# A decoder step on one core: two plain feed-forward tiles instead of three, right factors made in order of use, a norm's end counted in products, and one POOL product pinned in place

## The chip, the cores and the metric

The kernel runs on one core of a Trainium2 chip. The metric is the device time of one execution in microseconds (us). Five engines work side by side, each through its own list of instructions in a fixed order: TensorE (PE, with its weight loads shown as PEld), VectorE (DVE), ScalarE (ACT), GpSimd (POOL) and SyncE (SP), which starts the transfers.

## The reference, cut to what matters

One step of a two-layer decoder over 1024 prompt tokens and 8 decode rows (1032 columns), width 1024, everything in float32:

```python
for l in range(2):
    xn = modulate(h, norm_w[l, 0], sh1, sc1)         # rms_norm(h) * (1 + scale) + shift
    if l == 0:
        mix, s_new = hgrn2_mixer(xn, ...)            # gated linear recurrence, 8 heads
    else:
        mix = sliding-window attention over the shared K/V
    h = h + g1 * mix
    xn = modulate(h, norm_w[l, 1], sh2, sc2)
    h = h + g2 * swiglu(xn, w_ffn_in[l], w_ffn_out[l])   # d_ff = 2816
    if l == 0:
        k_sh, v_sh = modulate(h, kv_norm_w, ...) @ w_kv  # shared by layer 1
y = rms_norm(h, final_norm_w)
```

For a decode row, a head of the recurrence does `s_new = f * s + k v^T` on its 128 x 128 state, and its output is the query times that state.

## The kernel before, in words

**Products.** A float32 matrix product is made of three matmuls (`mm3`, L283 to L285) of operands split in a rounded high part and a low rest. A weight comes by a transfer to a `raw` buffer; ACT casts it (L182, the high part) and POOL subtracts (L185, the rest). The pairs stand in a ring of `RING = 8` units of 512 columns; most tiles are two units, and `ws.next()` writes the conversion of up to three tiles ahead of the one in use. The activations are split in the same way.

**Columns.** A layer's columns are worked through in chunks: four of 258 (`G4`) for the feed-forward's input side and the output projection, three of 344 (`G3`) for the rest.

**Feed-forward (`ffn`).** There are 22 tiles of 128 hidden channels, each with a gate and an up part. The first `PLAIN` tiles are plain products: two tiles together, chunk by chunk as each chunk of the normalised input becomes ready (`need`), and any further plain tile after them. The remaining tiles use seven products of half-size blocks in place of eight (`seven_products`, in the order 1, 2, 6, 7, 5, 3, 4). Their right factors (`xs7`) are blocks of the input (1, 2, 3) or sums of such blocks (4 to 7), which `factors` makes: `diff` subtracts two blocks on DVE (L1393), `part` splits the result (ACT cast L1388, DVE subtraction L1389). They overwrite the residual's stack `f`.

**A norm's end.** While the last products of a sub-layer run, each chunk's squares are summed (`square`: L783, L786, and L788 on DVE or POOL). `finish(c, before, after)` merges them on DVE (L801), lets `before` steps go by, sums over the partitions on PE (L714), takes the inverse root on DVE and makes a diagonal (L720), lets `after` steps go by and spreads it over the partitions on PE (L729). `apply_steps` then scales rows (L809), adds scale and shift on ACT, and splits (ACT, DVE L837). These pieces stand as generators in the list `later`; after each product the code calls `step()`, which takes the next piece of the first generator in the list that has real work, and also one of every generator that only counts (`LAG`). `flush` empties the list.

**Heads.** `run` interleaves generators by weights: while head h+1's projections (`hgrn_proj`) run, the core of head h (`hgrn_core`) runs beside them. A core goes through levels M = 1, 2, ... 64: PE (L1043, L1089, L1110), then DVE on queries and keys (L1064, L1065). `vb` is the decode rows' v, spread over the partitions by a round trip through DRAM (`vsc`), and POOL multiplies it with k (L1125). Later the decode states are updated (L1146), the outputs normalised (L1198), gated and sent to `osc` (L1214). The last head's core runs beside `wo_first`, the half of the output projection that needs heads 0 to 3; `conditioning` (L473) runs there too. `wo_first` takes four weight tiles at once, eight units. `wo_second` follows; it needs heads 4 to 7, loaded and split by `mixed` (L1301, L1302, L1304).

**Order.** The Python code gives a program order. A planner orders each engine's list ahead of the run from that order and from when it reckons operands to be ready, so a piece that is ready early can stand earlier than it was written. `tc.keep_in_program_order(i)` pins an instruction behind the last one that was written before it for its engine.

The K/V norm (`ToKV`) ends in the same way during the feed-forward's output products; `nkv.apply_steps` runs a second time to make the queries' input during the K/V products.

Of the kernel before, what the change touches and what calls it, by code (L numbers as in the profile page):

```python
# [12 lines left out]
ALU = mybir.AluOpType  # L13
# [4 lines left out]
P = 128  # L18
D = 1024
KT = 8  # L20
T = 1024
NB = 8
Q = 86
TOK = T + NB
# [6 lines left out]
RING = 8  # L31
RAW = 3
NSLOT = 34
PLAIN = 3
MAGIC = 0x5F3759DF


# [16 lines left out]
G3, G4 = Grid(344), Grid(258)  # L54
# [3 lines left out]
def bc(ap, axis, n):  # L58
    u = ap.unsqueeze(axis)
    shape = list(u.shape)  # L60
    shape[axis] = n
    return u.to_broadcast(shape)
# [3 lines left out]
def trunk_kernel(  # L66
# [40 lines left out]
    pe, act, dve, pool, sp = nc.tensor, nc.scalar, nc.vector, nc.gpsimd, nc.sync  # L107
# [14 lines left out]
    def big(dt=F32, cols=TOK, parts=P):  # L122
        return p4.tile([parts, cols], dt, tag="c4", name=nm("c4"))
# [14 lines left out]
    def small(shape, tag, bufs=2, dt=F32):  # L138
        return sm.tile(shape, dt, tag=tag, name=nm(tag), bufs=bufs)
# [74 lines left out]
    def ntile(w, n0):  # L214
        ws.add(
            split_unit(
                [
                    (
                        lambda r: r.rearrange("p (k n) -> p k n", k=KT),
                        w[:, n0 : n0 + P].rearrange("(k p) n -> p k n", p=P),  # L220
                    )
                ]
            ),
            2,
        )
# [6 lines left out]
    def seven(w, j):  # L232
        box = {}

        def load():
            for i in range(2):
                raw = wraw()
                v = raw.rearrange("p (g k n) -> p g k n", g=2, k=4)
                for g in range(2):
                    src = w[i * 512 : (i + 1) * 512, g * DFF + j * P : g * DFF + (j + 1) * P]  # L240
                    sp.dma_start(v[:, g], src.rearrange("(k p) n -> p k n", p=P))
                box[0, i] = raw[:, 0:512]
                box[1, i] = raw[:, 512:1024]

        def first():
            load()
            a11, a12, a21, a22 = box[0, 0], box[0, 1], box[1, 0], box[1, 1]
            u = weight(a11)
            s3 = wp.tile([P, 512], F32, tag="s3", name=nm("s3"), bufs=1)
            box["s3"] = s3  # L250
            dve.tensor_tensor(s3, a11, a21, op=ALU.subtract)
            dve.tensor_tensor(a21, a21, a22, op=ALU.add)
            dve.tensor_tensor(a11, a21, a11, op=ALU.subtract)
            return u

        def last_sum():
            s = box[0, 0]
            dve.tensor_tensor(s, box[0, 1], s, op=ALU.subtract)
            return weight(s)

        ws.add(first)
        ws.add(lambda: weight(box[0, 1]))
        ws.add(lambda: weight(box[0, 0]))
        ws.add(lambda: weight(box["s3"]))
        ws.add(lambda: weight(box[1, 0]))
        ws.add(last_sum)
        ws.add(lambda: weight(box[1, 1]))
# [71 lines left out]
    def ffn_units(l):  # L339
        for j in range(PLAIN):  # L340
            ntile(w_ffn_in[l], j * P)
            ntile(w_ffn_in[l], DFF + j * P)
        for j in range(PLAIN, NF):
            seven(w_ffn_in[l], j)
        for j in range(2):
            ktile(w_ffn_out[l], j)
        for j in range(2, NF, 4):
            for np_ in range(4):
                wo_pair(w_ffn_out[l], j, np_)
# [56 lines left out]
    for kk in range(4):  # L406
        t = big(cols=1024)
        wa[0].append(first_half(2 * kk, 0, t))
        t = big(cols=1024)
        wa[0].append(first_half(2 * kk + 1, 0, t))  # L410
    ws.ahead(3)
    for k in range(4):
        t = big(cols=1024)
# [141 lines left out]
    LAG = "lag"  # L555
# [4 lines left out]
        later.append([g, next(g) == LAG])  # L560

    def step(n=1):
        for _ in range(n):
            worked = False
            for e in list(later):
                if worked and not e[1]:
                    break
                r = next(e[0], None)
                if r is None:
                    later.remove(e)  # L570
                    continue
                e[1] = r == LAG
                worked = worked or not e[1]
# [56 lines left out]
    class Stack:  # L630
# [12 lines left out]
        def part(self, c, i, n):  # L643
            r = self.rows(i)
            return self.t[c][i][:, : r.stop - r.start, :n]
# [204 lines left out]
    def residual_dec(tdec):  # L850
        dve.tensor_tensor(hd, hd, tdec, op=ALU.add)


    N = Norm()
# [34 lines left out]
    for half in range(2):  # L889
# [5 lines left out]
            op=ALU.mult,  # L895
# [115 lines left out]
    def hgrn_core(hh):  # L1011
        f, kk, v, q, g = data.pop(hh)
# [5 lines left out]
        for half in range(2):  # L1018
            ps = axp()
            for j in range(4):  # L1020
                c = 4 * half + j
# [8 lines left out]
        vb = big(cols=T).rearrange("p (b v) -> p b v", b=NB)  # L1030
# [87 lines left out]
        for half in range(2):  # L1118
            ps = axp()
            for j in range(4):  # L1120
                c = 4 * half + j
                pe.transpose(ps[:, j * P : (j + 1) * P], KS[:, c * P : (c + 1) * P], ident)
            act.copy(kt[:, half * 512 : (half + 1) * 512], ps)

        pool.tensor_tensor(vb, vb, bc(kk[:, T:TOK], 2, P), op=ALU.mult)  # L1125
        yield
        S = big(cols=T)
        for half in range(2):
# [4 lines left out]
            for j in range(4):  # L1133
                c = 4 * half + j
# [25 lines left out]
        for half in range(2):  # L1160
            ps = axp()
            po.append(ps)
            for j in range(4):
                c = 4 * half + j
# [5 lines left out]
            for j in range(4):  # L1170
                c = 4 * half + j
# [25 lines left out]
        for half in range(2):  # L1197
# [4 lines left out]
                op=ALU.mult,  # L1202
# [4 lines left out]
        for half in range(2):  # L1207
            ps = axp()
            for j in range(4):
                c = 4 * half + j  # L1210
# [119 lines left out]
    def wo_second(o, gate, m, back, beside=iter(())):  # L1330
        tdec = small([P, KT, NB], "tdec", 2)
        us = [ws.next() for _ in range(4)]
        st = res[-1]
        N = StackNorm(st)
        x = Quads()

        def then(c):
            st.move(back, [c], False)
            yield from N.finish(c, *((3, 8) if c < G4.last else (2, 4)))
            yield LAG  # L1340
            yield from N.apply_steps(c, m, x)

        for c in range(G4.n):
            for n in range(KT):
                wo_product(us[n // 2], o, c, n, gate, tdec, G4, anyp)
                N.square(c, n)
                step()
                if c and ((c - 1) * KT + n) % 2 == 0:
                    next(beside, None)
            if c == G4.last:  # L1350
                residual_dec(tdec)
                N.square_dec()
            queue(then(c))
        for _ in beside:
            pass
        return x, st
# [18 lines left out]
    def factors(x, st):  # L1375

        x = x.q
        f = st.t  # L1380
        xs7 = [{1: x[2 * i][0], 2: x[2 * i][1], 3: x[2 * i + 1][1]} for i in range(2)]

        def flat(t):
            return t.rearrange("p k n -> p (k n)")

        def part(raw):
            xh, xl = quad()
            act.copy(xh, raw)  # L1388
            dve.tensor_tensor(xl, raw, xh, op=ALU.subtract)  # L1389
            return xh, xl  # L1390

        def diff(p, q, dst):
            dve.tensor_tensor(flat(dst), flat(p), flat(q), op=ALU.subtract)  # L1393
            return dst

        def steps():
            t2 = []
            for i in range(2):
                b11, b12, b22 = f[2 * i][0], f[2 * i + 1][0], f[2 * i + 1][1]
                t1 = diff(b12, b11, b11)  # L1400
                yield
                xs7[i][5] = part(t1)
                yield
                t2.append(diff(b22, t1, t1))
                yield
                xs7[i][6] = part(t2[i])
                yield
            for i in range(2):
                t3 = diff(f[2 * i + 1][1], f[2 * i + 1][0], f[2 * i + 1][0])
                yield  # L1410
                xs7[i][7] = part(t3)
                yield
            for i in range(2):
                t4 = diff(f[2 * i][1], t2[i], t2[i])
                yield
                xs7[i][4] = part(t4)
                yield

        return xs7, steps()

    def ffn(l, x, st, hs, norm, aside=None):
# [3 lines left out]
        xs7, prepare = factors(x, st)  # L1425

        def prepare_all():
            for _ in prepare:
                yield 1

        later.append([prepare_all(), False])

# [14 lines left out]
        for c in range(G4.n):  # L1447
            need(x, c)
            for i in range(2):
                gate(ui[2 * i], c, sg[i])  # L1450
                step()
                up(ui[2 * i + 1], c, sg[i])
                step()
        for i in range(2):
            sp.dma_start(act_out[i], sg[i])
        for j in range(2, PLAIN):
            sg = big()
# [71 lines left out]
        ready = []  # L1529
# [8 lines left out]

        for j in range(PLAIN, NF):
            if j == NF // 2 and aside:  # L1540
# [57 lines left out]
    class ToKV(StackNorm):  # L1598
# [12 lines left out]

        def then(self, c):
            self.st.move(hsc, [c], False)
            yield from self.finish(c, 3, 5)
            yield LAG
            yield from self.apply_steps(c, 2, self.x, keep=True)

# [9 lines left out]
    for c in range(NCH):  # L1627
        need(nkv.x, c)
        for n in range(4):
            ps = mmp()  # L1630
            proj(ps[:, :W], us[n], nkv.x, c)
            act.copy(kvT[n][:, G3.cs[c] : G3.cs[c] + W], ps[:, :W])
            step(2)
        later.append([nkv.apply_steps(c, 3, X, first=False), False])
    kT, vT = kvT[:2], kvT[2:]

# [2 lines left out]
    for a in range(2):  # L1639
        t = big(cols=T)  # L1640
# [411 lines left out]
```

## Time and profile before

| what | value |
|---|---|
| median of 3 runs | 2527.67 us (2525.5 to 2528.7) |
| profiled execution | 2529.57 us, span 2527.8 us |
| mean granted clock of TensorE | 0.992 |
| PE busy | 2469.5 us, 98% |
| DVE, ACT, POOL busy | 1366.9, 878.7, 797.3 us |

The span is the time between the first and the last instruction in the trace of the profiled execution; that execution's own time is the figure beside it. An engine's row gives the sum of its busy time. In timelines a row is: start, duration, engine, line, operation, output <- inputs, shape, and in brackets how long the engine stood idle just before and who ended that.

### The profile page before, as it was taken

What the parts mean: (1) busy time and instruction counts of PE and PEld (TensorE: products, weight loads), DVE (VectorE), ACT (ScalarE), POOL (GpSimd) and SP (SyncE); (2) the same over time, 40 slices, a digit from 0 to 9 for tenths busy, and PEclk for the clock granted to TensorE, in tenths of its full rate; (3) what the DMA queues carried; (4) which work ended last, traced back from release to release, by engine and by line L of the source; (5) the groups of instructions that cost most, each with busy time, mean ns of one, the idle gap of its engine ahead of it and who ended that gap; (6) DMA issues with size and microseconds to landing.
All of it is one profiled execution on the core that took longest, in us unless ns stands there. A gap on an engine that the chain in (4) does not pass through costs nothing.

```text
span 2527.8 us, 52251 instructions
## 1 busy us (share of the span) xinstructions
PE 2469.5 (98%) x21579; PEld 2346.0 (93%) x21579; DVE 1366.9 (54%) x3117; ACT 878.7 (35%) x1929; POOL 797.3 (32%) x577
## 2 busy tenths in 40 slices
PE   7999999999999999999999999999899999999998
PEld 4989999987889999999999997878899999999998
DVE  5444555564574555656433725566845555555436
ACT  4323333331363332333211655454633333333112
POOL 2211222220334444444432231102334444445321
PEclk9999999999999999999999999999999999999999
DMA  8564222248942223226321322523222222264201
GB/s 317 188 213 138 72 78 69 69 149 286 284 126 78 81 85 116 89 89 229 123 76 54 89 55 59 155 88 109 76 70 82 84 76 76 76 230 145 69 26 68
DMA packets 314495, 293.41 MB, mean 116 GB/s; under 512 B 28617, under 2 KB 291674, under 8 KB 314226
## 3 DMA queue, kind: packets, MB, share of 16 engines
q1 hardware_dynamic: 313856, 289.86, 35.5%
q8 instruction: 170, 2.79, 0.4%
q14 instruction: 67, 0.55, 0.1%
q10 hardware_dynamic: 402, 0.22, 0.0%
HBM read 231.27 MB, written 63.99 MB: 117 GB/s over the span
## 4 chain that ended last, share of the span: by engine, by line
PE 89%; DVE 5%; DMA 2%; issue 2%; SPq 1%; ACT 0%; POOL 0%; DVEq 0%; POOLq 0%; ACTq 0%
PE mm L283 20%; PE mm L285 20%; PE mm L284 20%; PE ax L283 6%; PE ax L284 6%; PE ax L285 6%; PE ax L473 2%; PE ax L1798 1%; PE ax L1869 1%; PE ax L1043 1%; PE ax L1855 1%; DVE c L1064 1%; PE ax L1132 1%; PE ax L1169 1%; DVE hs L809 1%
## 5 line engine op out<-in xcount | busy, mean ns | idle before, releaser
L185 POOL TENSOR_TENSOR wu<-raw,wu 128x512 fp32r<-128x512 f32 x460 | 626.2, 1368 | 1354.8 <-ACT wu L182 1118.7
L283 PE MATMUL mm<-c,wu 128*128 128x344 f32 (+1 forms) x2096 | 669.9, 320 | 6.0 <-ACT c L742 4.1
L285 PE MATMUL mm<-c,wu 128*128 128x344 f32 (+1 forms) x2096 | 658.7, 314 | 1.7 <-POOL wu L185 1.7
L284 PE MATMUL mm<-c,wu 128*128 128x344 f32 (+1 forms) x2096 | 658.7, 314 | 0.1
L182 ACT CAST wu<-raw 128x512 fp32r<-128x512 f32 x460 | 283.3, 620 | 705.9 <-PE mm L285 377.0
L283 PEld LDWEIGHTS mm<-c,wu 128*128 128x128 f32 x2096 | 395.6, 189 | 20.0 <-issue 10.3
L283 PE MATMUL mm<-xq,wu 128*128 128x258 f32 x1448 | 412.2, 285 | 1.0 <-ACT wu L182 1.0
L285 PE MATMUL mm<-xq,wu 128*128 128x258 f32 x1448 | 409.9, 283 | 0.8 <-POOL wu L185 0.8
L284 PE MATMUL mm<-xq,wu 128*128 128x258 f32 x1448 | 410.3, 283 | 0.0
L285 PEld LDWEIGHTS mm<-c,wu 128*128 128x128 f32 x2096 | 395.6, 189 | 6.2 <-issue 4.1
L284 PEld LDWEIGHTS mm<-c,wu 128*128 128x128 f32 x2096 | 396.2, 189 | 4.3 <-issue 3.4
L283 PE MATMUL ax<-xq,wu 128*128 128x258 f32 x1064 | 301.4, 283 | 0.0
L284 PE MATMUL ax<-xq,wu 128*128 128x258 f32 x1064 | 300.9, 283 | 0.0
L285 PE MATMUL ax<-xq,wu 128*128 128x258 f32 x1064 | 300.6, 283 | 0.0
L285 PEld LDWEIGHTS mm<-xq,wu 128*128 128x128 f32 x1448 | 275.2, 190 | 2.3 <-issue 1.2
L283 PEld LDWEIGHTS mm<-xq,wu 128*128 128x128 f32 x1448 | 274.5, 190 | 2.0 <-ACT wu L182 1.2
L284 PEld LDWEIGHTS mm<-xq,wu 128*128 128x128 f32 x1448 | 275.4, 190 | 0.1
L844 DVE SCALAR_TENSOR_TENSOR hs<-mm,ada,hs 128x344 f32<-128x344 f32 (+3 forms) x228 | 120.5, 532 | 183.8 <-PE mm L285 170.8
L284 PEld LDWEIGHTS ax<-xq,wu 128*128 128x128 f32 x1064 | 202.3, 190 | 0.0
L285 PEld LDWEIGHTS ax<-xq,wu 128*128 128x128 f32 x1064 | 201.6, 190 | 0.0
L283 PEld LDWEIGHTS ax<-xq,wu 128*128 128x128 f32 x1064 | 201.0, 189 | 0.0
L844 DVE SCALAR_TENSOR_TENSOR c<-mm,ada,c 128x344 f32<-128x344 f32 (+1 forms) x132 | 74.9, 571 | 111.3 <-PE mm L285 110.6
(323 smaller groups left out, 3596.1 us busy)
## 6 DMA issues: line engine op xcount, KB each, us to landing
c<-in_w_ada_dram SPq DMA_DIRECT2D x96, 512.0 KB
raw<-in_w_ffn_in_dram SPq DMA_DIRECT2D x152, 256.0 KB
ff<-c SPq DMA_DIRECT2D x44, 516.0 KB
c<-ff SPq DMA_DIRECT2D x44, 516.0 KB
raw<-in_w_ffn_out_dram SPq DMA_DIRECT2D x44, 512.0 KB
raw<-in_w_in_a_dram SPq DMA_DIRECT2D x32, 512.0 KB
hs<-hs SPq DMA_DIRECT2D x16, 516.0 KB
out_dram<-c SPq DMA_DIRECT2D x16, 512.0 KB
```

Of the source, the lines that this page charges most:

```text
L182: i = act.copy(u[:, 0, :], src)
L185: eng.tensor_tensor(u[:, 1, :], src, u[:, 0, :], op=ALU.subtract)
L283: pe.matmul(ps, wh, xh, start=first, stop=False)
L284: pe.matmul(ps, wh, xl, start=False, stop=False)
L285: pe.matmul(ps, wl, xh, start=False, stop=last)
L473: pe.matmul(ada_ps[q][32 * j : 32 * j + 32, 256 * i : 256 * i + 256], cT[:, k, :], u[i][:, j, :], start=(k == 0 and i == 0), stop=(k == KT ...
L809: dve.tensor_tensor(t, t, bc(R, 1, t.shape[1]), op=ALU.mult)
L844: dve.scalar_tensor_tensor(hc, ps[:, : g.pl[c]], ada[:, gate + n, 0:1], hc, op0=ALU.mult, op1=ALU.add)
L1043: pe.matmul(ps[32 * j : 32 * j + 32, c * 32 : (c + 1) * 32], KS[:, t0 : t0 + 32], QP[:, t0 : t0 + 32], start=True, stop=True, tile_positio ...
L1064: dve.tensor_tensor(q4[:, :, 1, :], q4[:, :, 1, :], bc(p3[:, :, 0], 2, M), op=ALU.mult)
L1132: pe.matmul(ps[:, j * P : (j + 1) * P], kt[:, s], vt[:, s], start=True, stop=True)
L1169: pe.matmul(o, attT[:, c, :], vt[:, s], start=(c == 0), stop=True)
```

## The change

- `PLAIN` goes from 3 to 2: the third plain feed-forward tile of each layer becomes a tile of seven products.
- `factors` waits for the chunks it reads, takes the differences by shorter formulas in another order (three for factor 6 first), and splits the factors in the order 6, 7, 5, 4.
- `step(n)`: a generator that only counts is advanced once in a call, not n times. In the feed-forward's first two tiles, each product of chunks 2 and 3 is followed by `step(3)`.
- The last chunk's norm before a feed-forward goes from distances (2, 4) to (3, 5); the K/V norm from (3, 5) to (4, 6), and after each K/V product two calls `step()` stand for one `step(2)`.
- L1125 is pinned in program order.

```diff
-PLAIN = 3
+PLAIN = 2
...
     def step(n=1):
-        for _ in range(n):
+        for t in range(n):
             worked = False
             for e in list(later):
+                if e[1] and t:
+                    continue
                 if worked and not e[1]:
                     break
...
-        pool.tensor_tensor(vb, vb, bc(kk[:, T:TOK], 2, P), op=ALU.mult)
+        tc.keep_in_program_order(pool.tensor_tensor(vb, vb, bc(kk[:, T:TOK], 2, P), op=ALU.mult))
...
-            yield from N.finish(c, *((3, 8) if c < G4.last else (2, 4)))
+            yield from N.finish(c, *((3, 8) if c < G4.last else (3, 5)))
...
-        x = x.q
+        ready, x = x.ready, x.q
...
         def steps():
-            t2 = []
             for i in range(2):
+                while not {2 * i, 2 * i + 1} <= ready:
+                    yield LAG
                 b11, b12, b22 = f[2 * i][0], f[2 * i + 1][0], f[2 * i + 1][1]
-                t1 = diff(b12, b11, b11)
+                diff(b12, b11, b11)
+                diff(b22, b12, b12)
                 yield
-                xs7[i][5] = part(t1)
+                diff(b22, b11, b22)
                 yield
-                t2.append(diff(b22, t1, t1))
-                yield
-                xs7[i][6] = part(t2[i])
+                xs7[i][6] = part(b22)
                 yield
             for i in range(2):
-                t3 = diff(f[2 * i + 1][1], f[2 * i + 1][0], f[2 * i + 1][0])
-                yield
-                xs7[i][7] = part(t3)
+                xs7[i][7] = part(f[2 * i + 1][0])
                 yield
             for i in range(2):
-                t4 = diff(f[2 * i][1], t2[i], t2[i])
+                xs7[i][5] = part(f[2 * i][0])
                 yield
-                xs7[i][4] = part(t4)
+            for i in range(2):
+                diff(f[2 * i][1], f[2 * i + 1][1], f[2 * i][1])
+                yield
+                xs7[i][4] = part(f[2 * i][1])
                 yield
...
         def prepare_all():
-            for _ in prepare:
-                yield 1
+            for r in prepare:
+                yield r or 1
...
                 gate(ui[2 * i], c, sg[i])
-                step()
+                step(1 if c < 2 else 3)
                 up(ui[2 * i + 1], c, sg[i])
-                step()
+                step(1 if c < 2 else 3)
...
-            yield from self.finish(c, 3, 5)
+            yield from self.finish(c, 4, 6)
...
-            step(2)
+            step()
+            step()
```

## The prediction

> **What bounds the kernel now.** I read the page first (engines, the chain that ended last), then TensorE's waits, then windows over the stretches that the diff touches, and there the timelines of PE, DVE and POOL with what released each wait.
>
> ```profile
> span 2527.8 us, 52251 instructions
> PE 2469.5 (98%) x21579; PEld 2346.0 (93%) x21579; DVE 1366.9 (54%) x3117; ACT 878.7 (35%) x1929; POOL 797.3 (32%) x577
> ...
> PE 89%; DVE 5%; DMA 2%; issue 2%; SPq 1%; ACT 0%; POOL 0%; DVEq 0%; POOLq 0%; ACTq 0%
> ```
>
> PE is busy for 98% of the span and is 89% of the chain. So the time moves in two ways only: PE gets fewer matmuls, or a place where PE stands still is opened or closed. All other engines are half idle; their work counts where PE waits for it. PE's waits by line:
>
> ```profile
> PE ax L714 <- DVE sq L801: 8.8, 5, 5.8
> PE ax L1043 <- DVE c L1065: 8.1, 7, 1.8
> ...
> PE ax L729 <- DVE w L720: 1.6, 1, 1.6
> ```
>
> The columns are total us, times, longest. L714 and L729 are the two PE steps of a norm's end, whose places the diff moves. L1043 is the HGRN2 core, where the diff pins a POOL product. The windows give the price of a product and of a cold clock (us, busy of PE with its matmuls in brackets, then PEld, DVE, ACT, POOL, the granted clock, DMA share, GB/s):
>
> ```profile
> 733.08:786.67 53.59, 53.59 (x447) 53.56 (x445) 30.35 (x38) 25.09 (x43) 15.28 (x12) 1.00 0.15 50
> 786.67:806.80 20.13, 20.13 (x170) 20.13 (x169) 10.01 (x21) 6.49 (x13) 8.99 (x8) 1.00 0.28 90
> 1822.40:1875.84 53.44, 53.44 (x447) 53.41 (x446) 29.42 (x37) 23.34 (x39) 14.77 (x12) 1.00 0.16 51
> 1808.00:1812.00 4.00, 4.00 (x20) 4.00 (x21) 2.59 (x6) 0.01 (x1) 0.00 (x0) 0.50 0.34 102
> 1812.00:1815.00 3.00, 3.00 (x20) 2.88 (x20) 1.63 (x3) 0.76 (x2) 0.00 (x0) 0.77 0.03 5
> 1436.00:1445.00 9.00, 8.90 (x51) 8.91 (x52) 5.45 (x17) 6.90 (x13) 0.00 (x0) 0.81 0.23 51
> ```
>
> The first and third are the end of the plain FFN tiles of layers 0 and 1, the second the first seven-product tile. PE is without a hole in all three, one matmul each 53.59/447 = 0.120 us.
>
> **The change, part by part** (minus is faster).
>
> *1. PLAIN 3 to 2: -5.7.* A plain tile has 2 x 4 x 8 x 3 = 192 matmuls, a seven-product tile 7 x 2 x 4 x 3 = 168. 24 fewer at 0.120 us are 2.88 us a layer, 5.75 us for two. The extra weight sums go to DVE, ACT and POOL, which in the seven-product window are busy 10.0, 6.5 and 9.0 of 20.1 us, so they cost nothing. What could be late is a right factor: product 6 now starts two products (48 x 0.120 = 5.8 us) after the seven products begin, 7, 5 and 4 at +8.6, +11.5 and +17.3 us, and they begin 22.9 us earlier than before.
>
> ```profile
> L1388 ACT CAST xq<-hs x16: 1035/1053/1061, 722.4 to 1860.3; 128x1032 fp32r<-128x1032 f32 x16
> ```
>
> Layer 1's last cast starts at 1860.3 and its seven products now start at 1875.84 - 22.9 = 1852.9; the last factor is wanted at 1870.2, and the order of use puts 6 first. I take 0; upper end +3, two casts and two subtractions late.
>
> *2. The FFN entry of layer 1: -3.*
>
> ```profile
> 1798.19 1.22 DVE L1393 TENSOR_TENSOR hs<-hs,hs 128x1032 f32<-128x1032 f32 x1
> ...
> 1800.94 1.84 DVE L1393 TENSOR_TENSOR hs<-hs,hs 128x1032 f32<-128x1032 f32 x1
> ...
> 1801.05 0.29 PE L285 MATMUL mm<-xq,wu 128*128 128x258 f32 x1
> ...
> 1802.70 2.29 DVE L837 TENSOR_TENSOR xq<-hs,xq 128x1032 fp32r<-128x1032 f32 x1
> ...
> 1804.91 1.73 DVE L788 TENSOR_TENSOR sq<-sq,sq 128x500 f32<-128x500 f32 x1
> ...
> 1806.70 0.41 DVE L801 TENSOR_TENSOR sq<-sq 128x250 f32<-128x250 f32 x1
> ...
> 1807.16 0.59 PE L714 MATMUL ax<-ones,sq 128*86 128x1 f32 x3 [5.83 <-DVE sq L801]
> ```
>
> PE ends its last product at 1801.34 and stands until 1807.16 for the last chunk's sum of squares, which is late behind DVE's differences and subtractions. Then it runs at a clock of 0.50 for 4 us and 0.77 for 3 us: 2.0 + 0.7 us lost besides. Moving L714 from two products to three puts 24 matmuls more (2.87 us) ahead of it: the gap falls to about 3. Three differences now stand in one step where two stood ahead of L801, so up to one more (1.22) can stand there, and part of the clock loss stays or goes. I take -3; ends: 0 (DVE later by as much as PE) and -8.5 (gap and clock loss both gone). The row nearest is the gap itself, 5.83 - 2.87, so I stay near it.
>
> The Trainium skill ("TensorE: Matmul & The Clock Gate", section "Why this matters for your kernels") says that the clock falls back only after PE gaps of more than about 3 us. By that rule the shortened gap costs no clock and this term is -5.6, the sum 2.6 lower. The window at 1436 above speaks against it: a clock of 0.81 for 9 us, after gaps of no more than 1.6 and 1.65 us (rows in part 4).
>
> *3. The FFN entry of layer 0: -0.8.* The five waits of L714 are 8.8 us; without the 5.83 and the KV norm's 1.65, what is left for layer 0 and elsewhere is 1.3. Ends 0 and -1.3.
>
> *4. The KV norm (3,5 to 4,6; two calls of one step): -1.*
>
> ```profile
> 1424.98 0.51 DVE L720 TENSOR_TENSOR w<-ident,ny 86x344 f32<-86x344 f32 x1
> ...
> 1425.64 0.53 PE L729 MATMUL ax<-w,ones 86*128 86x344 f32 x1 [1.60 <-DVE w L720]
> ...
> 1429.62 0.43 PE L284 MATMUL mm<-xt,wu 128*128 128x344 f32 x1 [0.15 <-DVE xt L837]
> ...
> 1436.10 0.39 PE L714 MATMUL ax<-ones,sq 128*86 128x1 f32 x3 [1.65 <-DVE sq L801]
> ```
>
> Here a matmul has 344 columns instead of 258, about 0.120 x 344/258 = 0.16 us, and a product 12 of them, 1.9 us (ffn-out), or 24, 3.8 us (K/V). L729 of the second chunk moves behind the first K/V product, so its 1.60 goes. L714 of the third chunk keeps its PE place, so its 1.65 stays. Against that, the first chunk's L729 comes two ffn-out products (3.8 us) later, and everything from there to its factors with it; the row at 1429.62 shows that the first K/V product already waits 0.15 for its last factor. Up to 3.8 us come back here. I take half of it, 1.9, and 1.3 off the clock loss (9 x 0.19 = 1.7): -1.60 + 1.9 - 1.3 = -1. Ends -4 and +3.
>
> *5. The pinned product in heads 0 to 6: +7.5.* L1125 multiplies the decode state's rows on POOL.
>
> ```profile
> 331.51 1.28 POOL L185 TENSOR_TENSOR wu<-raw,wu 128x512 fp32r<-128x512 f32 x1 [2.28 <-ACT wu L182]
> ...
> 331.97 1.37 DVE L1064 TENSOR_TENSOR c<-c,c 128x512 f32<-128x512 f32 x1 [1.76 <-PE ax L1089]
> ...
> 333.26 0.68 DVE L1065 TENSOR_TENSOR c<-c,c 128x512 f32<-128x512 f32 x1
> ...
> 334.09 1.12 PE L1110 MATMUL ax<-c,c 128*64 128x64 f32 x16
> ```
> ```profile
> L1125 POOL TENSOR_TENSOR c<-c,c x8: 1898/2060/2442, 111.6 to 574.1; 128x1024 f32<-128x1024 f32 x8
> ...
>   DMA c<-vsc: 42.1, 4
> ```
> ```profile
> 574.09 0.69 DVE L1064 TENSOR_TENSOR c<-c,c 128x512 f32<-128x512 f32 x1 [1.20 <-PE ax L1043]
> 574.09 2.44 POOL L1125 TENSOR_TENSOR c<-c,c 128x1024 f32<-128x1024 f32 x1 [18.78 <-DMA c<-vsc]
> ...
> 574.69 2.38 DVE L1065 TENSOR_TENSOR c<-c,c 128x512 f32<-128x512 f32 x1
> ```
>
> The last fence shows what L1125 does to DVE: L1065, 0.69 us when alone, takes 2.38 beside it, and ends with it. Before, L1125 starts when its load lands. Pinned, it stands behind the last POOL instruction written before it, the second weight subtraction of the next head's tile 1 (here 331.51 to 332.79). So it runs from about 333, on L1064 and L1065, whose results L1110 wants at 334.09: L1065 ends near 336.0 instead of 333.94, and PE waits 1.9 us. The same pattern stands in cores 2 to 6: 5 x 1.9 = 9.5, and 0.4 in core 0; in core 1 the subtraction lies clear of such a pair. Behind L1125 on POOL stands only the next tile's subtraction, which waits for its own cast. Off go the old collisions with L1043, about 1.0 in each of cores 1 and 2 (the seven waits of L1043 for L1065 are 8.1/7 = 1.2 each). +9.9 - 2.0 = +7.9, taken as +7.5. Ends -2 (L1125 falls in a free slot) and +10.
>
> *6. The pinned product in the last head's tail: +4.*
>
> ```profile
> 631.28 2.52 POOL L185 TENSOR_TENSOR wu<-raw,wu 128x512 fp32r<-128x512 f32 x2 [54.75 <-ACT wu L182]
> ...
> 640.36 1.29 POOL L185 TENSOR_TENSOR wu<-raw,wu 128x512 fp32r<-128x512 f32 x1
> ...
> 607.38 2.18 DVE L1146 SCALAR_TENSOR_TENSOR c<-c,c,c 128x128 f32<-128x128 f32 x8
> ...
> 617.66 0.34 SPq L1214 DMA_DIRECT2D osc<-c  x1
> ...
> 642.25 0.28 PE L283 MATMUL ax<-c,wu 128*128 128x258 f32 x1
> ```
> ```profile
> L473 PE MATMUL ax<-c,cT x160: 379/379/403, 617.8 to 662.0; 128*32 128x256 f32 x160
> ...
> 655.26 1.93 PE L473 MATMUL ax<-c,cT 128*32 128x256 f32 x32
> ```
>
> The last head's core runs beside `wo_first`, which holds all eight weight buffers; the subtractions of tiles 4 to 6 are written ahead of L1125 and cannot start until its last chunk frees them. That is the 54.75 us of idle POOL. So L1125 goes from 574 to about 641. From L1146 to the store of the head's rows is 10.6 us (607.38 to 618.0); with 2 for L1125 and some 5 for the store, the load and the split (an estimate; the head's cast and subtraction alone are 1), the rows are there near 659. `wo_second` starts at 642.25 and each of its products wants head 7 as its last quarter: it is late by 659 - 643 = 16 us. PE's cover: nine matmuls (1.08 us) of a product for each free bank, 4 to 8 of them, 4.3 to 8.6 us; the core's own PE work, 2; conditioning (L473), 160 matmuls of 1.93/32 = 0.06 us, 9.6 us, so far as it is free to wait. Full cover is 16 to 20, poor cover 6. Behind L1125 on POOL stand tile 7's subtractions, 2 us later than before, wanted only by the last two products of a chunk. I take 11 covered of 16, less the 1.4 of the old collision at 574: about +4. Ends -1.4 and +12 (10 open, and 2 at a cold clock).
>
> **Sum.** -5.7 - 3 - 0.8 - 1 + 7.5 + 4 = +1.0. The profiled execution took 2529.6 us (span 2527.8), 1.9 above the median of 2527.7; +1.0 on the median is 2528.7.
>
> **Rivals.**
> - *The pins find room* (faster). L1125 slips between DVE's pairs (part 5: -2, as in core 1), and the tail is covered (part 6: -1.4): 2527.7 - 10.5 - 3.4 = 2514; with only one of the two, 2518 to 2523. For it: PE's order in the tail is free. Against it: POOL is idle when the subtraction ends, so nothing holds L1125 back from the bad moment.
> - *The FFN entry closes wholly*, gap and clock, -8.5 instead of -3, the rest as forecast: 2523. For it: differences now wait for their chunks. Against: L837 and L788 (2.29 and 1.73) are still ahead of L801.
> - *The tail opens* (slower). PE stands behind the first head-7 quarter with little ahead of it: +12 instead of +4: 2537. It decides when less than 6 of the 16 us are covered; that happens if the conditioning waits for banks which the core's late results hold.
> - *The longer distances starve the first K/V product*: +3 instead of -1, and the FFN entry gains nothing: 2536. For it the 0.15 at 1429.62; against it: only its last factor is late there, so the first two thirds of the product have slack.
> - *The change does nothing where it is put*: the pin leaves L1125 where it was (as in core 0, where it already runs behind its weights) and only part 1 counts: 2522.
>
> **How the numbers follow.** A difference under 0.2% (5 us) can't be told from none. My forecast, parts 5 and 6 about eating what parts 1 to 4 give, has 0.44 and its own range 2523 to 2533. The pins find room 0.18, FFN entry closes 0.06, pin without effect 0.06; tail opens 0.16, starved K/V 0.10. Of the two cases near 2522 a part lies within 5 us: faster 0.27, within 0.47, slower 0.26. The range runs from 2517 (one pin harmless and parts 1 to 4 as summed) to 2539 (tail open, and part 5 at its upper end).
>
> **What would show it.** Part 1: 24 matmuls fewer in each FFN, seven products starting some 23 us earlier against the FFN's start, no PE wait for L1388 or L1389. Part 2: L714's longest wait near 3 instead of 5.8. Part 4: no wait for L720, a new one for L837 of up to 4. Part 5: L1125 directly behind a weight subtraction, and a new wait of PE L1110 for L1065 of 1.9, five times. Part 6: the last L1125 near 640, and a hole in PE between 642 and 660. I am wrong if L1110 has no wait, or if PE has no hole in the tail, or if L1125 runs late without anything waiting for it.

## The result, and the profile after

The changed kernel takes 2540.3 us (median; 2536.5 to 2545.7) against 2526.6 us before: a ratio of 1.0055, 95% interval 1.0035 to 1.0076. It is slower by 13.7 us, outside the forecast range (2517 to 2539), on the side to which I gave 0.26. The profiled execution took 2541.15 us.

The page of the changed kernel: the span, the engines, the chain that ended last.

```profile
span 2539.3 us, 52247 instructions
PE 2467.8 (97%) x21531; PEld 2340.1 (92%) x21531; DVE 1402.9 (55%) x3153; ACT 882.5 (35%) x1939; POOL 808.5 (32%) x583
...
PE 87%; DVE 5%; DMA 3%; issue 2%; SPq 1%; ACT 1%; POOL 0%; DVEq 0%; POOLq 0%; ACTq 0%
```

PE has 48 matmuls fewer (21531 against 21579) and yet a longer span: it stands still more, 71.5 us of the span against 58.3, and its mean granted clock is 0.990 against 0.992. (The lines from L560 on that are named here moved by two: L1125 is L1127 now, L1110 is L1112, L714 is L716, L729 is L731, L837 is L839.) Its waits, by line:

```profile
PE ax L1112 <- DVE c L1071: 9.2, 5, 1.8
PE ax L1045 <- issue: 8.2, 3, 3.5
...
PE ax L1045 <- DVE c L1067: 5.1, 5, 1.0
PE ax L1213 <- DVE c L1200: 4.6, 1, 4.6
...
PE ax L716 <- DVE sq L803: 4.2, 4, 2.5
PE ax L1180 <- DVE c L1148: 3.3, 1, 3.3
...
PE mm L284 <- DVE xt L839: 2.0, 1, 2.0
...
PE ax L716 <- DVE sq L796: 1.2, 1, 1.2
```

Three kinds are new: L1112 in five heads, L1180 and L1213 in the last head's tail, L839 in the K/V norm (0.2 before). The 8.2 of L1045 stand in the last head, where before had 4.3 and 1.4; the profile doesn't show what it waits for, and e3 below has 3.2 there. L716 has shrunk from a longest wait of 5.8 to 2.5. The first kind in the timeline of one head:

```profile
333.06 1.29 POOL L185 TENSOR_TENSOR wu<-raw,wu 128x512 fp32r<-128x512 f32 x1 [2.34 <-ACT wu L182]
334.30 2.35 POOL L1127 TENSOR_TENSOR c<-c,c 128x1024 f32<-128x1024 f32 x1
...
334.82 2.38 DVE L1067 TENSOR_TENSOR c<-c,c 128x512 f32<-128x512 f32 x1
...
337.35 0.82 PE L1112 MATMUL ax<-c,c 128*64 128x64 f32 x11 [1.83 <-DVE c L1071]
```

L1127 stands directly behind the weight subtraction. L1067, 0.7 us when alone, takes 2.38 beside it and ends 0.55 us after it (337.20 against 336.65). What follows differs from head to head. Windows behind L1112 of heads 2 to 6 (us, PE, PEld, DVE, ACT, POOL, granted clock, DMA):

```profile
272.30:277.70 5.40, 5.40 (x25) 5.40 (x25) 1.37 (x3) 0.58 (x1) 0.00 (x0) 0.68 0.00 0
338.40:342.30 3.90, 3.90 (x27) 3.88 (x26) 1.37 (x3) 0.58 (x1) 0.00 (x0) 1.00 0.02 4
402.90:408.40 5.50, 5.50 (x33) 5.37 (x32) 1.37 (x3) 0.58 (x1) 0.00 (x0) 0.77 0.01 3
469.10:472.90 3.80, 3.80 (x25) 3.80 (x25) 1.37 (x3) 0.58 (x1) 0.00 (x0) 1.00 0.00 0
533.60:539.20 5.60, 5.60 (x41) 5.54 (x38) 1.89 (x4) 2.05 (x4) 0.00 (x0) 1.00 0.01 3
```

After the same wait the clock fell in two heads of five. Two falls cost 5.40 x 0.32 + 5.50 x 0.23 = 3.0 us; from one L1112 to the next it is 66.1 us behind a fall and 64.6 without one. L1112 of head 6 comes at 532.6 us and not at 522.7.

The tail of the changed kernel: PE, the product on POOL, SP, and on ACT the row that ends the conditioning (L484) with the first split behind it. The last row is the window with the granted clock.

```profile
645.55 0.90 PE L1180 MATMUL ax<-c,qz 128*32 128x128 f32 x4 [3.31 <-DVE c L1148]
...
655.84 1.94 PE L1213 MATMUL ax<-ident,c 128*128 128x128 f32 x8 [4.63 <-DVE c L1200]
...
658.14 8.72 PE L473 MATMUL ax<-c,cT 128*32 128x256 f32 x128
```
```profile
642.23 1.90 POOL L1127 TENSOR_TENSOR c<-c,c 128x1024 f32<-128x1024 f32 x1
```
```profile
574.89 2.64 SPq L1303 DMA_DIRECT2D w<-osc  x3
...
647.36 0.38 SPq L1157 DMA_DIRECT2D out_dram<-c  x1
647.84 3.06 SPq L276 DMA_DIRECT2D c<-in_w_ada_dram  x4
658.60 0.34 SPq L1216 DMA_DIRECT2D osc<-c  x1
```
```profile
666.93 0.59 ACT L484 COPY c<-ax 128x512 f32<-128x512 f32 x1 [14.62 <-PE ax L473]
667.41 0.48 ACT L1304 CAST c<-w 128x344 fp32r<-128x344 f32 x1
```
```profile
644.40:661.40 17.00, 11.22 (x65) 6.03 (x69) 9.89 (x33) 1.55 (x6) 2.21 (x2) 0.50 0.76 237
```

L1127 runs at 642 (forecast: about 641; why that is luck stands below). The first rows of heads 4 to 6 are loaded from 574.9 us on (L1303), but split only behind L484. `wo_second` has its first product at 667.98 us, against 642.25 before. 12.2 of these 25.7 us stand already at L1112 of the last head; the tail adds 13.5: PE stands still for 8.7 of them (3.31, 4.63 and 0.72 ahead of L488), and the rest falls into 17 us at a clock of 0.50. From there on the changed kernel wins back 14.8, so that its last PE instruction is 10.95 us later than before's.

### The profile page after: what moved, and what is told of

The parts are those of the page before. It is cut to its first block, busy times and chain, and to the rows that moved or that the text cites. A ratio compares the mean times of both kernels' runs of the same rounds, so it can differ in the third digit from the quotient of the medians.

```text
span 2539.3 us, 52247 instructions
## 1 busy us (share of the span) xinstructions
PE 2467.8 (97%) x21531; PEld 2340.1 (92%) x21531; DVE 1402.9 (55%) x3153; ACT 882.5 (35%) x1939; POOL 808.5 (32%) x583
## 4 chain that ended last, share of the span: by engine, by line
PE 87%; DVE 5%; DMA 3%; issue 2%; SPq 1%; ACT 1%; POOL 0%; DVEq 0%; POOLq 0%; ACTq 0%
PE mm L283 20%; PE mm L285 19%; PE mm L284 19%; PE ax L283 6%; PE ax L284 6%; PE ax L285 6%; PE ax L1802 1%; PE ax L473 1%; PE ax L1873 1%; PE ax L1045 1%; PE ax L1859 1%; DMA c<-in_w_ada_dram 1%; DVE c L1066 1%; DVE c L1067 1%; PE ax L1134 1%
## 5 line engine op out<-in xcount | busy, mean ns | idle before, releaser
L185 POOL TENSOR_TENSOR wu<-raw,wu 128x512 fp32r<-128x512 f32 x464 | 634.6, 1375 | 1418.4 <-ACT wu L182 1106.9
L283 PE MATMUL mm<-xq,wu 128*128 128x258 f32 x1376 | 391.4, 284 | 1.3 <-ACT wu L182 1.0
L285 PE MATMUL mm<-xq,wu 128*128 128x258 f32 x1376 | 389.7, 283 | 0.8 <-POOL wu L185 0.8
L284 PE MATMUL mm<-xq,wu 128*128 128x258 f32 x1376 | 389.7, 283 | 0.0
L283 PE MATMUL ax<-xq,wu 128*128 128x258 f32 x1120 | 316.7, 283 | 0.0
L284 PE MATMUL ax<-xq,wu 128*128 128x258 f32 x1120 | 315.8, 282 | 0.0
L285 PE MATMUL ax<-xq,wu 128*128 128x258 f32 x1120 | 315.0, 281 | 0.0
L283 PEld LDWEIGHTS mm<-xq,wu 128*128 128x128 f32 x1376 | 260.8, 190 | 2.6 <-ACT wu L182 1.2
L285 PEld LDWEIGHTS mm<-xq,wu 128*128 128x128 f32 x1376 | 260.8, 190 | 2.3 <-issue 1.2
L284 PEld LDWEIGHTS mm<-xq,wu 128*128 128x128 f32 x1376 | 261.6, 190 | 0.1
L284 PEld LDWEIGHTS ax<-xq,wu 128*128 128x128 f32 x1120 | 212.1, 189 | 0.0
L285 PEld LDWEIGHTS ax<-xq,wu 128*128 128x128 f32 x1120 | 211.6, 189 | 0.0
L283 PEld LDWEIGHTS ax<-xq,wu 128*128 128x128 f32 x1120 | 211.5, 189 | 0.0
```

Source lines behind the costliest of these rows:

```text
L185: eng.tensor_tensor(u[:, 1, :], src, u[:, 0, :], op=ALU.subtract)
L283: pe.matmul(ps, wh, xh, start=first, stop=False)
L284: pe.matmul(ps, wh, xl, start=False, stop=False)
L285: pe.matmul(ps, wl, xh, start=False, stop=last)
```

## The experiments

The theory from this profile (P): the pin alone costs the time, in the heads and in the tail; the rest of the change gains what was forecast.

**The pin taken out, put in alone, and split by place.** Four kernels on one chip.

```diff
 e1:  changed kernel,  L1127 without keep_in_program_order
 e2:  kernel before,   L1125 with keep_in_program_order
 e3:  changed kernel,  pinned only if hh < NH - 1
 e4:  changed kernel,  pinned only if hh == NH - 1
```

> The changed kernel with the decode product L1127 no longer pinned; all else as changed. Theory P (the pin alone costs the time, in two places): +12 us in heads 0 to 6 and +13.5 us in the last head's tail go, the gains of the other parts stay: about 2526.6 - 16 = 2511 us, no PE wait of L1112, wo_second's first product 25 us earlier than in the changed kernel. Rival R (the other parts cost time and the pin is neutral): about 2540 us, as the changed kernel. Rival Q (the late pieces only moved the wait): 2520 to 2530.

Measured: 2516.9 us, ratio to before 0.9958 (0.9946 to 0.9971).

> The kernel before with nothing changed but the pin of L1125. Theory P: 2526.6 + 25 = about 2552 us, five PE waits of L1110 of 1.8 us, and a hole in PE of over 10 us ahead of wo_second. Rival R: 2526 to 2528. Rival Q: 2535 to 2545, since the last head's delay is in part made up before the feed-forward.

Measured: 2551.6 us, 1.0096 (1.0082 to 1.011).

> The changed kernel with the pin in heads 0 to 6 only; the last head's product is free. Theory P: 2511 + 12 = about 2523 us, with the five waits of L1112 but no hole ahead of wo_second. If the heads cost only their five waits without the colder clock behind them: 2511 + 8 to 9 = 2520. Rival (the tail is what costs, heads are absorbed): 2511 to 2514.

Measured: 2527.1 us, 0.9999 (0.999 to 1.0008).

> The changed kernel with the pin in the last head only. Theory P: 2511 + 13.5 = about 2525 us, no wait of L1112, the last L1127 at about 630 us (10 us earlier, since the heads are faster) and the hole ahead of wo_second as in the changed kernel. Rival (the hole needs the delay of the heads as well): 2511 to 2516.

Measured: 2530.1 us, 1.0014 (1.0004 to 1.0023).

Before is 2527.3 us in these comparisons, and 2526.6 to 2527.3 in all others on two further chips, so I set times of different comparisons side by side. Without the pin the change gains 10.4; the pin in the heads costs 10.2 on top of that (2527.1 - 2516.9), in the tail 13.2 (2530.1 - 2516.9). Together 2516.9 + 23.4 = 2540.3, the changed kernel's time; and alone on the kernel before the pin costs 24.2. So the two places add up, and rivals R and Q of these expectations are out. e1 missed its own number: I had put its gain at 16 from the trace's stretches. The waits of e1 (pin taken out) and of e4 (pin in the tail only):

```profile
PE ax L1045 <- DVE c L1067: 6.7, 7, 1.2
...
PE ax L716 <- DVE sq L803: 4.3, 4, 2.5
...
PE mm L284 <- DVE xt L839: 2.0, 1, 2.0
...
PE ax L716 <- DVE sq L796: 1.5, 1, 1.5
```
```profile
PE ax L1215 <- DVE c L1202: 4.6, 1, 4.6
...
PE ax L1182 <- DVE c L1150: 3.3, 1, 3.3
```

No L1112 in either, and in e4 the tail's two waits are the same 4.6 and 3.3, under its own line numbers. L1112 of heads 2 to 6 in e3 (pin in the heads only):

```profile
271.09 1.12 PE L1112 MATMUL ax<-c,c 128*64 128x64 f32 x16 [1.78 <-DVE c L1071]
...
335.69 1.12 PE L1112 MATMUL ax<-c,c 128*64 128x64 f32 x16 [1.77 <-DVE c L1071]
...
400.27 1.12 PE L1112 MATMUL ax<-c,c 128*64 128x64 f32 x16 [1.80 <-DVE c L1071]
...
464.88 1.12 PE L1112 MATMUL ax<-c,c 128*64 128x64 f32 x16 [1.78 <-DVE c L1071]
...
529.46 1.12 PE L1112 MATMUL ax<-c,c 128*64 128x64 f32 x16 [1.77 <-DVE c L1071]
```

The same five waits, 64.6 us apart each time: here the clock fell behind none of them. In e1 L1112 of head 6 comes at 522.5 us, so that the waits by themselves cost 6.9 us by head 6. The other 3.3 of the 10.2 don't stand at them in this trace; in it the clock falls at 997 and at 1540 us, where e1's doesn't; e1 has one fall, at 1424 us, that e3 has not. The mean granted clock is 0.992 to 0.994 in the executions of e3 and 0.994 to 0.996 in those of e1. Whether the pin has a part in that is not shown.

**Why the tail: nothing written ahead.**

```diff
     def wo_first(...):
+        if not before_last:
+            ws.look = 0
         us = [ws.next() for _ in range(4)]
+        ws.look = RING - 2
```

> The changed kernel, pin and all, but the first half of the output projection in layer 0 writes no weight conversions ahead (tiles 4 to 6 are converted from wo_second's first call on). So the last head's L1127, still pinned, has no waiting subtraction ahead of it on POOL. Theory P1 (the tail's cost is L1127 standing behind subtractions that wait for buffers): L1127 of the last head at about 590 us and not 642, the hole ahead of wo_second gone, 2540.3 - 13.2 = about 2527 us, up to 2 us more if the later conversions hold wo_second up. Rival (the pin itself, through the order of the chain behind it, makes the hole): about 2540 us.

Measured: 2528.1 us, 1.0002 (0.9994 to 1.0011). The product is still pinned, but POOL's list no longer has the waiting subtractions ahead of it:

```profile
581.92 1.90 POOL L1127 TENSOR_TENSOR c<-c,c 128x1024 f32<-128x1024 f32 x1 [18.21 <-DMA c<-vsc]
639.11 2.52 POOL L185 TENSOR_TENSOR wu<-raw,wu 128x512 fp32r<-128x512 f32 x2 [55.29 <-ACT wu L182]
```

12.3 us of the tail's 13.2 are gone. It is what stands ahead of the product, and not the pin as such.

**Why the heads: the product's length, and its engine.**

```diff
 e6:  pool.tensor_tensor(vb[:, 0:4], vb[:, 0:4], bc(kk[:, T : T + 4], 2, P), op=ALU.mult), pinned
 e7:  for b in range(NB):
          act.activation(vb[:, b, :], vb[:, b, :], AF.Copy, scale=kk[:, T + b : T + b + 1]), each pinned
```

> The changed kernel with L1127 working on half of its columns (128x512 instead of 128x1024; decode rows 4 to 7 are left unmultiplied). Theory P2 (DVE's L1067 cannot run while POOL's L1127 holds what they share, so PE's wait at L1112 is as long as L1127 lasts): L1127 takes 1.2 instead of 2.35 us, the five waits of L1112 shrink from 1.8 to 0.6 to 0.8 us each, and with them the colder clock behind them: 5 to 8 us faster than the changed kernel, about 2533 to 2535. Rival (a signal or an order between POOL and DVE makes the wait, whatever L1127's length): waits of 1.8 us stay, 2539 to 2541.

Measured: 2532.4 us, 1.0017 (1.0009 to 1.0026), 8 less than the changed kernel. The groups and a window behind the wait:

```profile
L1127 POOL TENSOR_TENSOR c<-c,c x8: 1045/1488/1496, 126.5 to 631.8; 128x512 f32<-128x512 f32 x8
```
```profile
PE ax L1112 <- DVE c L1071: 4.6, 5, 0.9
```
```profile
335.00:339.00 4.00, 4.00 (x27) 3.95 (x26) 1.37 (x3) 0.58 (x1) 0.00 (x0) 1.00 0.08 23
```

L1127 is 0.86 us shorter (1.49 against 2.35) and the wait 0.92 (4.6/5 against 9.2/5): PE waits as long as POOL holds DVE up. The clock stays at 1.00 behind all five waits (one is shown), but so it does in e3 behind waits of 1.8 us, so this run doesn't show that the shorter wait spares the clock. The Trainium skill ("SBUF — State Buffer", section "Who interferes with whom") says that a DVE instruction with two SBUF inputs contends with a GpSimd one that reads SBUF, for ports that are locked to one of the two at a time. The trace agrees: L1067 ends about its own 0.7 us after L1127, and the step is 0.86 and 0.92 us.

> The changed kernel with the decode product, still pinned, made by eight ACT instructions of 128x128 (scale by a column) in place of one POOL instruction. Theory P: neither cost is left, no wait of L1112 and no hole ahead of wo_second, 2540.3 - 23.4 = about 2517 us as without the pin, and down to 2514 if the collisions ahead of L1045 go as well. Rival (the late place of the product, on any engine, is what costs): 2530 to 2540; ACT is delayed by some 2 to 3 us per head ahead of its cast of weights, which would show as a PE wait for L182 or L1115.

Measured: 2520.1 us, 0.9972 (0.9961 to 0.9983): pinned at the same place of the program, but no wait of L1112, none in the tail, and `wo_second` at 643.1 us. The eight ACT instructions last 0.39 us each. In the last head they begin at 595.4 us at the latest and not at 642, so on ACT's list the place is not as late in time. The pin costs little (3.2 us more than without it) where the product shares neither POOL's queue with the weights nor time with DVE.

**The other parts.**

```diff
 e8:   kernel before,  PLAIN = 2
 e10:  changed kernel without the pin,  K/V norm finish(c, 3, 5) and step(2) as before
 e11:  changed kernel without the pin,  (2, 4) in place of (3, 5) ahead of a feed-forward
 e12:  changed kernel without the pin,  K/V norm finish(c, 4, 5)
```

> The kernel before with only PLAIN = 2; factors, distances and the free L1125 as before. If part 1 is 24 matmuls less a layer and nothing else: 2527.3 - 5.7 = 2521.6 us. Rival (the old order of factors is too late for seven products that begin 23 us earlier): PE waits for L1388 or L1389 ahead of product 6, and 2523 to 2530.

Measured: 2522.1 us, 0.9978 (0.9969 to 0.9986): -5.1, with no wait for L1388 or L1389. The old order of factors was not late either.

> The changed kernel without the pin and with (2, 4) in place of (3, 5) for the last chunk ahead of a feed-forward; factors as changed. If the distance makes part 2 (PE arriving 2.9 us later at the same sum of squares): the wait of L716 in layer 1 goes from 2.5 and 1.5 back to about 5, 2516.9 + 2.3 to 3 = about 2519.5 us. Rival (the new factors move DVE's work out of the way, and the distance is nothing): 2516 to 2518.

Measured: 2520.5 us, 0.9974 (0.9965 to 0.9984). The long wait is back:

```profile
PE ax L716 <- DVE sq L803: 8.1, 4, 5.8
```

So the distance gives 3.6 (2520.5 - 2516.9), and the new factors alone don't.

> The changed kernel without the pin and with the K/V norm's distances and steps as before (3, 5; one step(2)). If part 4 is worth what the traces show (-1.8 us between the feed-forward's output and the K/V products): 2516.9 + 1.8 = about 2518.7 us; the waits of L731 for L722 (1.6) and of L716 (1.65) are back, the wait of 2.0 for L839 is gone. Rival (the wait for L839 and the cold clock behind it eat the gain): 2515 to 2517.

Measured: 2525.0 us, 0.9993 (0.9984 to 1.0002), a miss of both theories. Its waits:

```profile
PE mm L283 <- ACT xt L838: 4.2, 1, 4.2
...
PE ax L731 <- DVE w L722: 1.6, 1, 1.6
```

The 1.6 is back and the 2.0 for L839 gone (0.2), as expected, but the 1.65 of L716 is not back, and the 4.2 is new, and in neither kernel above. I read it so: with the new counting a `step(2)` advances a norm that only counts once, not twice, so the old distances under one `step(2)` make later ends than they did before. This kernel is therefore not the old norm, and part 4's own price stays with the traces: from one product of the feed-forward's output (1407.82 us before, 1404.72 in e1) to the third K/V chunk (1446.21 and 1441.29) it is 38.4 us before and 36.6 in e1, -1.8, with the wait for L839 inside.

> The changed kernel without the pin and with (4, 5) for the K/V norm: L731 of the first chunk comes one product earlier (1.9 us) than with (4, 6), that of the second still behind the first K/V product. If the 2.0 us wait for L839 and the cold clock behind it come from the first chunk's L731 being two products late: the wait goes to about 0.1 to 0.5 and 2516.9 - 2 to 4 = 2513 to 2515 us. Rival (the wait is DVE's own lateness): about 2517 us.

Measured: 2518.3 us, 0.9967 (0.9957 to 0.9977); no gain, and the wait for L839 is 2.2. So the wait does not come from the first chunk's L731 being two products late. The time fits the rival; where the wait does come from is not settled.

**Why the tail's delay found no cover.** I moved first the splits of heads 4 to 6, then the conditioning (in e13 and e14 quads 3 to 6 take each other's weights, since these come in a fixed order; the work is the same).

```diff
 e9:   + o2 = mixed(osc, 1, ks=range(3))      # ahead of run(wo_first, hgrn_tail, conditioning)
       - o = mixed(osc, 1)
       + o = mixed(osc, 1, o2, (3,))
 e13:  run((wo_first, 16), (hgrn_tail, 28));  wo_second(..., conditioning((6, 3, 4, 5), (2, 3, 4)))
 e14:  e13 and e9
```

> The changed kernel, pin and all, but the rows of heads 4 to 6 that wo_second reads are loaded and split ahead of the last head's core; only head 7's come after it. Theory P3 (the 16 us of delay in the tail found less cover than I counted, since heads 4 to 6 were split only behind the conditioning's end on ACT, so no product of wo_second could begin): PE now runs 33 to 36 matmuls of wo_second (4 banks) ahead of L1213, the wait of 4.6 us there goes, and the slow start of wo_second too: 5 to 8 us faster than the changed kernel, 2532 to 2535 us. Rival (heads 4 to 6 were there, and banks or PE's order held the products): 2539 to 2541.

Measured: 2542.5 us, 1.0066 (1.0052 to 1.0079). P3 falls: the wait at L1213 is down to 0.9, and some 33 matmuls of `wo_second` stand ahead of it, but nothing is gained. The stretch behind it:

```profile
657.54 0.64 PE L473 MATMUL ax<-c,cT 128*32 128x256 f32 x8 [1.70 <-DMA c<-in_w_ada_dram]
...
664.97 1.08 PE L473 MATMUL ax<-c,cT 128*32 128x256 f32 x8 [0.42 <-DMA c<-in_w_ada_dram]
666.75 1.11 PE L488 MATMUL ax<-ident,c 128*128 128x128 f32 x4 [0.71 <-ACT c L484]
```

The conditioning now waits for its own weights, and `wo_second`'s next products behind L488 begin at 667.5 us, as in the changed kernel.

> The changed kernel, pin and all, with the conditioning of quads 4 and 5 moved from beside the last head's core to beside wo_second (they are wanted only in layer 1). Theory P4 (the conditioning that I had counted as cover was itself held: its transfers stand behind the late core's stores on SP, and its end, L484 and L488, stands ahead of wo_second's splits and products on ACT and PE): wo_second's first product comes at 655 to 660 us and not at 668; the 160 or so matmuls moved cost their 10 us again inside wo_second, so the total is 2538 to 2543 us. Rival (head 7's rows, their store, load and split, set the start): the first product stays at 665 or later, total 2546 or more.

Measured: 2563.6 us, 1.0141 (1.0126 to 1.0156).

> As the kernel with the conditioning moved, and the rows of heads 4 to 6 loaded and split ahead of the last head's core. Theory P4: now 33 to 36 matmuls of wo_second run ahead of L1213, with nothing behind them that waits for transfers: about 4 us faster than the one without, 2534 to 2538 us. Rival (the rows bring nothing, as in the run that had them with the conditioning left in place): equal to the one without, within 2 us.

Measured: 2553.7 us, 1.0106 (1.0088 to 1.0123).

P4 is right in kind on the start, wrong on the total. In e13 the product L1127 comes at 623.5 us and `wo_second`'s first matmul 5.9 us after it (629.4), against 25.8 us in the changed kernel (forecast: 13 to 18, with L1127 at 642): 36 of its matmuls run ahead of L1213, the next at 639.6. The splits of heads 4 to 6 that these need now come long before. So the conditioning did hold `wo_second`'s start. But its transfers, moved behind, are late again. ACT, SP and PE of e13, and a window with the granted clock, the DMA share and GB/s at its end:

```profile
591.25 0.48 ACT L1304 CAST c<-w 128x344 fp32r<-128x344 f32 x1
```
```profile
658.02 21.59 SPq L276 DMA_DIRECT2D c<-in_w_ada_dram  x16
```
```profile
PE ax L473 <- DMA c<-in_w_ada_kv_dram: 6.8, 10, 1.8
PE ax L473 <- DMA c<-in_w_ada_dram: 6.1, 13, 0.9
```
```profile
730.00:768.00 38.00, 26.16 (x201) 6.71 (x202) 0.74 (x5) 2.16 (x3) 0.20 (x1) 0.57 1.08 349
```

16 transfers take 21.6 us to issue, 1.35 each, and PE waits for them again and again: conditioning goes at the pace of its transfers. In the window of 38 us the DMA share is 1.08 at 349 GB/s, PE stands still for 11.8 us, and its clock is at 0.57. The early rows are worth 9.9 us there (2563.6 - 2553.7) and nothing where the conditioning stands in front. It isn't P4's reason that makes them worth that: the 36 matmuls ahead of L1213 run in e13 already. Where the 9.9 us come from is not settled. Part of the cover's failure stays open: how early the conditioning's weights could have come was not tried.

## Why the prediction was wrong, point by point

- *Parts 1 to 4* (-5.7, -3, -0.8, -1: -10.5). Measured together -10.4 (e1). Part 1 is -5.1, part 2's distance alone -3.6 with a longest wait of 2.5 and not 5.8, part 4 -1.8 in the trace, its new wait for L839 included (2.0; forecast: up to 4). Part 3 brought nothing: the waits of layer 0's entry are 0.6 us before and 1.1 in e1. The sum is nearer than its parts. Some of it is the clock, with a mean of 0.994 to 0.996 in e1's executions and of 0.991 to 0.994 in before's.
- *Part 5* (+7.5, ends -2 and +10). The mechanism was right to the row: L1127 directly behind the subtraction, five waits of 1.8 us (forecast 1.9). The old collisions that I took off at 2.0 came off at 1.8 in the changed kernel: L1112 of head 1 comes 1.0 us earlier than before, and that of head 2 at the same time although it holds its own wait. In the trace of e3 this leaves 6.9 us against e1. The total was 10.2, just above my upper end: I put nothing down for the clock, which costs 3.0 us behind the waits in the changed kernel's trace and elsewhere in e3's.
- *Part 6* (+4, ends -1.4 and +12). The step that failed. That L1127 moves to the end of `wo_first` was right, but 642 against 641 is luck. The 642 holds the 12.2 us that had gathered by the last head; with the heads free (e4) L1127 runs at 629.3, since `wo_first`, with the conditioning and the late core behind it, leaves PE at 629.3 and not at 642. From L1127 to the store of head 7's rows it is 16.4 us in both (642.2 to 658.6, 629.3 to 645.6), and I had counted 12.6. What failed is the cover, which I put at 11 of 16 us. `wo_second` begins 12.0 us later in e4 than in e1 (654.0 against 642.0), and the cost was 13.2, above my upper end. I counted 9.6 us of conditioning and up to 8.6 us of early products as free work. But the products need splits that stand on ACT behind the conditioning's end (L484, then L1304), and the conditioning needs transfers that stand on SP behind the late core's own stores (L1157, then L276; the last is issued at 650.4 us and lands 6.9 later). Both were in line behind the piece that was late. My rival "the tail opens" named the price (+12) and the condition (under 6 us covered); I gave it 0.16. Its reason, banks held by the late results, was not tested by itself.
- The sum: 10.2 - 7.5 and 13.2 - 4 make 11.9 of the 11.6 us between 2540.3 and 2528.7.
- *The clock.* The Trainium skill ("TensorE: Matmul & The Clock Gate", section "Why this matters for your kernels") asks for no PE gap over about 3 us. Here a gap of 1.8 us was followed by a clock of 0.68 and 0.77 in two heads and of 1.00 in three, and in e3 of 1.00 in all five. The measurement decides: gaps well under 3 us can cost the clock, though not each time.

The version without the pin (e1, 2516.9 us) beats both kernels.

## What to carry to other kernels

A pin behind "what was written before" takes over the fate of whatever that is: read which instruction it is in each place, and what that one waits for. Five of eight places here put the product against DVE's busiest moment, one put it behind buffers that came free some 60 us later (642.2 against 581.9 us in e5). And work counts as cover for a delay only if none of its queues (transfers, casts, PE's list) has the late piece ahead of it; follow each of them before taking it off the price.

## What the runs showed of the hardware

- Whether PE's clock falls after a gap of 1.8 us is a matter of chance, as far as these traces show. Seven traces have the five equal gaps (the changed kernel, e2, e3, e5, e9, e13, e14), and it fell behind 7 of the 35 (2, 1, 0, 1, 2, 1, 0), for 1.5 us each. None fell behind the five gaps of 0.9 us in e6, which is too few to tell the two lengths apart.
- The executions of one kernel differ by such falls. Those of the changed kernel took 2536.5, 2539.5, 2541.2 and 2545.7 us at a mean granted clock of 0.992, 0.991, 0.990 and 0.989: 0.003 of 2540 us is 7.6 of the 9.2 us between them.
- POOL's product on 128x1024 takes 1.90 us alone and 2.35 beside DVE's two-input products, which take up to 2.38 and not 0.69: both engines pay.
